# Who reads the split weight tile before a weight sum's DMA, and at which loads the values' sums are issued, in a hybrid decoder block

## The chip, the cores and the metric

One core of a Trainium2 chip runs the kernel in one launch. The metric is the device time of the whole program in microseconds, the median of several executions. Beside the times there is one profiled execution, with a page of summary views and a trace that can be asked for its waits, its chain, its transfers and any stretch of its timeline.

## The reference

The reference is one decoder layer on a sequence of 256 tokens with a model width of 1024. It is cut here to what matters for the order of the work:

```python
proj = jnp.einsum('bsd,dn->bsn', x, w_in)                  # 1024 x 9216 weights
hq, hf, hi, hg, mq, mk, mv, gate_logits = jnp.split(proj, offsets, axis=-1)
o_a = hgrn2_mixer(hq, hf, hi, lb)                          # gated linear recurrence, 8 heads
y_a = rms_norm(o_a, hgrn_norm_w) * silu(hg)
y_b = moba_attention(apply_rope(mq), apply_rope(mk), mv)   # causal attention, 8 heads
z_a, z_b = y_a @ w_branch_a, y_b @ w_branch_b
g_a, g_b = split(sigmoid(gate_logits + b_gate), 2)
x = layer_norm(DN_ALPHA * x + (g_a * z_a + g_b * z_b) @ w_out, ln1_w, ln1_b)
h_gate, h_up = split(x @ w_ffn_in, 2)
return layer_norm(DN_ALPHA * x + (silu(h_gate) * h_up) @ w_ffn_down, ln2_w, ln2_b)
```

All of it is float32. The two projections that this case touches are `hg` (columns 3072 to 4095 of `w_in`), the gate of the recurrence, and `mv` (columns 6144 to 7167), the values of the attention.

## The kernel before

**Weights.** All weights lie in HBM as blocks of 128 x 2048 float32, 1 MB each, in the array `wts`. The kernel walks a list of 89 loads in a fixed order; `stage` (L222 to L250) does one. The SP queue issues the DMA of the block into a tile `raw` (L238; three buffers, so the load three places on is issued when the split of this one is done), ScalarE casts it into a rounded high part `wh` (L243), and VectorE subtracts to get the low part `wl` (L245). `wh` and `wl` have four buffers each, so load n+4 writes the buffers of load n (further on they shift by two, where two loads have tiles of their own). TensorE multiplies with high and low parts for float32 accuracy. I call the cast and the subtraction the split of a load.

**Fewer products.** The gate projection, the values projection and the down projection are done as 2 x 2 block products with seven instead of eight block multiplications (L619 to L658 for gate and values). Some of their right sides are sums and differences of quarters of the weights, called `u1` to `u4`. These sums are not made by an engine but by DMA: the GpSimd queue copies one weight block into a scratch block in HBM, and then copies another block onto it with an adding DMA (L264, `accum_op`). A product that needs `u3` then simply loads it like any other block (`raw<-u` in the profile, `raw<-in_wts_dram` for the plain ones). The list `SUMS` names eight steps for a full set of sums; the gate projection has eight, the values projection four (`u3` copied, `u2` copied, a block added to `u3`, then `u3` added to `u2`), and the down projection sixteen. They are 28 in all, and I number them 0 to 27 in the order of issue: 0 to 7 for the gate, 8 to 11 for the values, 12 to 27 for the down projection.

**When a sum is issued.** `SUMS_WITH` holds 28 load numbers. When `stage` has split load n and n stands in that list, it calls `sum_weights` with the first column of `wl` (L249, L250). That function lets VectorE copy this column of 128 numbers into a small tile `ticks` (L261), lets GpSimd add the tick to itself into `mark` (L262), and puts the DMA behind it on GpSimd's queue (L264). The value of `mark` is never used: the addition is there so that GpSimd's queue stands still until that load is split, and the DMA is not issued before. The additions and DMAs of GpSimd stay in the order in which they are written (`keep_in_program_order`). Where a sum reads what an earlier sum wrote, GpSimd's queue waits for that DMA to land before it issues the next.

The loads that matter here are: 14, 15, 17 and 22, the gate's `u1`, `u3`, `u2` and `u4`; 26 (values `u3`) and 28 and 33 (values `u2`), which need sums 10 and 11; 18, a plain block for the gate; 64 to 71 in the feed-forward part; and 74 on, the down projection.

**Order of the work.** The program is built by a scheduler that simulates a timeline (L1128) and orders the instructions of each engine by it, except in three stretches written out by hand (`manual_schedule`: the first projection, the end of the branches with the first norm, and the down projection) and for the instructions that are kept in program order. Between about 52 us and 205 us VectorE does the steps of the recurrence (`hgrn_steps`, L486 to L568: the steps `kl`, `Qt`, `Kt`, `Tt`, `SD` in the profile) between the splits of the loads, while TensorE runs the projections `hi`, `gb`, `hg`, `ga`, `mv`, `mk`, `mq`.

Of the kernel before, what the change touches and what calls it, by code (L numbers as in the profile page):

```python
# [10 lines left out]
F32 = mybir.dt.float32  # L11
# [3 lines left out]
ALU = mybir.AluOpType  # L15
PSUM = bass.MemoryType.PSUM

P = 128
# [25 lines left out]
VALUE_PRODUCTS = (11, "u1", "u3", "u2", 22, 21, "u4")  # L44
VALUES_BEHIND = (1, 2, 3, 4)
DOWN_ORDER = (0, 1, 3, 4, "a", 2, 6, "b", "c", 5)
SUMS_WITH = (2, 3, 4, 5, 6, 7, 8, 9, 11, 12, 13, 15,
             38, 39, 40, 41, 56, 57, 58, 59, 60, 61, 62, 63, 64, 65, 66, 67)
SUMS = (("u3", 12), ("u1", 11), ("u2", 11), ("u3", 22, "add"), ("u1", 12, "add"), ("u4", 21),
        ("u2", "u3", "add"), ("u4", "u2", "add"))  # L50
# [99 lines left out]
def hybrid_layer_kernel(ctx: ExitStack, tc, x, xw, vecs, wts, ln1_w, ln1_b, ln2_w, ln2_b, consts, out):  # L150
    nc = tc.nc
    pool = lambda name, bufs, **kw: ctx.enter_context(tc.tile_pool(name=name, bufs=bufs, **kw))
    cp = pool("cp", 1)
# [14 lines left out]
    def r32(ap):  # L168
        return ap.bitcast(F32)
# [31 lines left out]
    _, loads, sums = plan()  # L201
    mixed_weights = {}

    def source(at):
        if not isinstance(at, tuple):
            return wts[at]
        if at not in mixed_weights:
            mixed_weights[at] = tc.dram_tile([P, 2048], F32, name=f"{at[3]}_{at[2]}_{at[1]}")
        return mixed_weights[at]
# [12 lines left out]
    def stage(pieces=None, eng=nc.vector):  # L222
        i = state["next"]
        if i >= len(loads):
            return
        state["next"] += 1
        at, k, held = loads[i]
        src = source(at).rearrange("p (k c) -> p k c", k=k)
        view = lambda z: z.rearrange("p (k c) -> p k c", k=k)
        home, tag = (late, "late") if state.get("four") and i % 4 == 0 else (wraw, "raw")  # L230
        raw = view(home.tile([P, 2048], F32, tag=tag, name=f"raw{i}"))
        if held is True:
            h, l = view(slot(f"wh{i}", F32R)), view(slot(f"wl{i}", F32R))
        else:
            h = view(whi.tile([P, 2048], F32R, tag="h", name=f"wh{i}"))
            l = view(wlo.tile([P, 2048], F32R, tag="l", name=f"wl{i}"))
        for ks in ks_of(pieces or (k,)):
            load = nc.sync.dma_start(raw[:, ks, :], src[:, ks, :])  # L238
            if i < EARLY:
                tc.keep_in_program_order(load)  # L240
            if held == "onto":
                nc.vector.tensor_add(raw[:, ks, :], raw[:, ks, :], state["raw"][:, ks, :])
            nc.scalar.copy(h[:, ks, :], raw[:, ks, :])  # L243
            yield
            eng.tensor_sub(l[:, ks, :], raw[:, ks, :], r32(h[:, ks, :]))  # L245
            yield
        state["raw"] = raw
        ready.append((h, l))
        for _ in range(SUMS_WITH.count(i)):  # L249
            sum_weights(r32(l[:, 0, 0:1]))  # L250

    mark = cp.tile([P, 1], F32, tag="mark", name="mark")
    ticks = cp.tile([P, len(sums)], F32, tag="ticks", name="ticks")

    def sum_weights(behind):


        n = len(SUMS_WITH) - len(sums)
        dst, src, add = sums.pop(0)
        tick = ticks[:, n:n + 1]  # L260
        nc.vector.tensor_copy(tick, behind)  # L261
        tc.keep_in_program_order(nc.gpsimd.tensor_tensor(mark, tick, tick, op=ALU.add))  # L262
        more = dict(accum_op=ALU.add, max_dma_last_dim=2048) if add else {}
        tc.keep_in_program_order(nc.gpsimd.dma_start(source(dst), source(src), **more))  # L264

# [728 lines left out]
    for j in range(EARLY, NF, 2):  # L994
        n = j // 2 % 2
# [138 lines left out]
```

## Time and profile before

| | |
|---|---|
| median of 3 runs (lowest to highest) | 491.88 us (491.52 to 492.25) |
| the profiled execution's own time | 492.5 us |
| its span, first to last instruction | 490.7 us |
| TensorE (PE) busy | 482.1 us, 98% of the span |
| VectorE (DVE) busy | 402.9 us, 82% |
| ScalarE (ACT) busy | 318.3 us, 65% |
| GpSimd (POOL) busy | 60.1 us, 12% |

The profiled execution lies 0.6 us above the median. Of its time 1.8 us lie outside the span. Times in the views are in us from the start of the span. In a row of the timeline the first number is the start, the second the length; the bracket at the end is the idle time of that engine before it and what ended it. The letter q behind an engine's name means its queue (a DMA issue or a wait, not work). Instructions follow one another in a pipeline, so a row can begin a little before the one ahead of it has ended.

### The profile page before, as it was taken

How to read it: one execution, taken by the hardware profiler on the slowest of the kernel's cores; microseconds unless marked ns; L12 is line 12 of the kernel's file. 1: busy time of each engine (PE TensorE's matmuls, PEld its weight loads, DVE VectorE, ACT ScalarE, POOL GpSimd, SP SyncE). 2: the span in 40 equal slices, each digit the busy share in tenths (PEclk: the TensorE clock that was granted, in tenths of full speed). 3: DMA queues.
4: the chain of work that ended last, by engine and by line, in shares of the span. 5: the costliest groups of instructions: out<-in, count | busy, mean ns of one | idle time of the engine just before them, and what ended most of it. 6: DMA issues, size and time to landing. Idle time of an engine off the chain costs nothing.

```text
span 490.7 us, 7353 instructions
## 1 busy us (share of the span) xinstructions
PE 482.1 (98%) x2892; PEld 429.6 (88%) x2892; DVE 402.9 (82%) x496; ACT 318.3 (65%) x453; POOL 60.1 (12%) x81
## 2 busy tenths in 40 slices
PE   9999999999999999999999999999999999999993
PEld 9999888888888998999888888888888888888883
DVE  4888899999899789799875998855886679668796
ACT  5797676765879779689773565444665656568610
POOL 2305150320000010001010000001213011000000
PEclk9999999999999999999999999999999999999998
DMA  8979999999957764859767276249999999979902
GB/s 298 387 267 427 280 290 346 285 350 327 296 220 253 285 230 178 311 199 343 257 258 258 85 262 242 97 176 410 282 309 353 316 310 306 294 284 385 344 1 87
DMA packets 23986, 133.60 MB, mean 272 GB/s; under 512 B 2352, under 2 KB 2480, under 8 KB 12336
## 3 DMA queue, kind: packets, MB, share of 16 engines
q1 hardware_dynamic: 15264, 100.63, 53.8%
q0 software_dynamic: 8688, 32.51, 25.8%
q8 instruction: 23, 0.38, 0.3%
q14 instruction: 11, 0.09, 0.1%
HBM read 132.08 MB, written 30.41 MB: 331 GB/s over the span
## 4 chain that ended last, share of the span: by engine, by line
PE 85%; DVE 10%; DMA 2%; issue 1%; ACT 1%; DVEq 0%
PE fu L323 7%; PE fg L323 7%; DVE wl L245 4%; PE fg L324 3%; PE fu L324 3%; PE zb L323 3%; PE za L323 3%; PE ga L323 2%; PE wd L1037 2%; PE wd L1039 2%; PE wd L1038 2%; DMA raw<-in_wts_dram 2%; PE hf L395 2%; PE hf L396 2%; PE hq L367 2%; PE hq L366 2%
## 5 line engine op out<-in xcount | busy, mean ns | idle before, releaser
L245 DVE TENSOR_TENSOR wl<-raw,wh 128x2048 fp32r<-128x2048 f32 x89 | 202.7, 2290 | 54.4 <-ACT wh L243 54.3
L243 ACT CAST wh<-raw 128x2048 fp32r<-128x2048 f32 x89 | 169.5, 1914 | 61.0 <-PE fg L323 17.5
L323 PE MATMUL fg<-x1p,wh 128*128 128x512 f32 x144 | 50.5, 394 | 0.0
L323 PE MATMUL fu<-x1p,wh 128*128 128x512 f32 x144 | 50.4, 394 | 0.0
L324 PE MATMUL fg<-x1p,wl 128*128 128x256 f32 x144 | 40.0, 277 | 0.0
L324 PE MATMUL fu<-x1p,wl 128*128 128x256 f32 x144 | 39.9, 277 | 0.0
L262 POOL TENSOR_TENSOR mark<-ticks 128x1 f32<-128x1 f32 x28 | 21.5, 768 | 134.7 <-DVE ticks L261 111.8
L323 PEld LDWEIGHTS fu<-x1p,wh 128*128 128x128 f32 x144 | 27.0, 187 | 6.2
L323 PEld LDWEIGHTS fg<-x1p,wh 128*128 128x128 f32 x144 | 27.0, 187 | 6.1
L324 PEld LDWEIGHTS fg<-x1p,wl 128*128 128x128 f32 x144 | 27.0, 188 | 0.1
L324 PEld LDWEIGHTS fu<-x1p,wl 128*128 128x128 f32 x144 | 27.0, 188 | 0.0
L323 PE MATMUL za<-yP,wh 128*128 128x512 f32 x64 | 23.6, 405 | 0.0
L323 PE MATMUL ga<-xP,wh 128*128 128x512 f32 x64 | 22.8, 398 | 0.0
L323 PE MATMUL gb<-xP,wh 128*128 128x512 f32 x64 | 22.7, 397 | 0.0
L323 PE MATMUL zb<-yb,wh 128*128 128x512 f32 x64 | 22.3, 394 | 0.0
L365 PE MATMUL mq<-xP,wh 128*128 128x256 f32 x64 | 18.6, 290 | 0.0
L367 PE MATMUL mk<-xP,wl 128*128 128x256 f32 x64 | 18.5, 289 | 0.0
L264 POOL DMA_DIRECT2D u<-in_wts_dram x21 | 17.2, 817 | 10.0 <-DMA u<-in_wts_dram 7.9
L365 PE MATMUL mk<-xP,wh 128*128 128x256 f32 x64 | 18.4, 287 | 0.0
L324 PE MATMUL za<-yP,wl 128*128 128x256 f32 x64 | 18.3, 285 | 0.0
L366 PE MATMUL mq<-xP,wh 128*128 128x256 f32 x64 | 18.2, 284 | 0.0
L366 PE MATMUL mk<-xP,wh 128*128 128x256 f32 x64 | 18.2, 284 | 0.0
(339 smaller groups left out, 1360.0 us busy)
## 6 DMA issues: line engine op xcount, KB each, us to landing
raw<-in_wts_dram SPq DMA_DIRECT2D x74, 1024.0 KB, 6.5
raw<-u SPq DMA_DIRECT2D x15, 1024.0 KB, 7.3
u<-in_wts_dram POOLq DMA_DIRECT2D x7, 1024.0 KB, 17.1
u<-u POOLq DMA_DIRECT2D x7, 1024.0 KB, 17.7
first<-in_xw_dram SPq DMA_DIRECT2D x6, 640.0 KB, 9.7
xr<-in_x_dram POOLq DMA_DIRECT2D x1, 1024.0 KB, 5.4
wb<-in_ln_w_dram POOLq DMA_DIRECT2D x2, 512.0 KB, 6.3
wb<-in_ln_b_dram POOLq DMA_DIRECT2D x2, 512.0 KB, 7.7
```

The source lines that it names most:

```text
L243: nc.scalar.copy(h[:, ks, :], raw[:, ks, :])
L245: eng.tensor_sub(l[:, ks, :], raw[:, ks, :], r32(h[:, ks, :]))
L262: tc.keep_in_program_order(nc.gpsimd.tensor_tensor(mark, tick, tick, op=ALU.add))
L264: tc.keep_in_program_order(nc.gpsimd.dma_start(source(dst), source(src), **more))
L323: nc.tensor.matmul(ps, wh[:, k, wcol], a.both(k), start=(k == 0), stop=False)
L324: last = nc.tensor.matmul(ps[:, 0, :], wl[:, k, wcol], a[0, k, slice(0, T)], start=False, stop=(k == KC - 1))
L365: nc.tensor.matmul(ps, wh[:, k, wcol], ah[:, kk, :], start=(kk == 0), stop=False)
L366: nc.tensor.matmul(ps, wh[:, k, wcol], al[:, kk, :], start=False, stop=False)
L367: nc.tensor.matmul(ps, wl[:, k, wcol], ah[:, kk, :], start=False, stop=(kk == KC - 1))
L395: nc.tensor.matmul(pss[f], wh[:, wcol], xTh[:, k, :], start=(k == 0), stop=False)
L396: nc.tensor.matmul(pss[f], wh[:, wcol], xTl[:, k, :], start=False, stop=False)
L1037: nc.tensor.matmul(ps, lh[:, k, :], wh[:, k, ns], start=n < 5 and i + k == 0, stop=False, **go)
```

## The change

Two things are changed. `sum_weights` no longer copies the column into `ticks`: GpSimd's addition reads the column of `wl` itself, as both of its inputs. And four entries of `SUMS_WITH` move: the values' four sums (8 to 11) were paced by loads 11, 12, 13 and 15, and are now paced by loads 13, 15, 17 and 20. The other 24 entries, the sums and their order stay as they are.

```diff
-SUMS_WITH = (2, 3, 4, 5, 6, 7, 8, 9, 11, 12, 13, 15,
+SUMS_WITH = (2, 3, 4, 5, 6, 7, 8, 9, 13, 15, 17, 20,
              38, 39, 40, 41, 56, 57, 58, 59, 60, 61, 62, 63, 64, 65, 66, 67)
...
-    ticks = cp.tile([P, len(sums)], F32, tag="ticks", name="ticks")
...
     def sum_weights(behind):
-        n = len(SUMS_WITH) - len(sums)
         dst, src, add = sums.pop(0)
-        tick = ticks[:, n:n + 1]
-        nc.vector.tensor_copy(tick, behind)
-        tc.keep_in_program_order(nc.gpsimd.tensor_tensor(mark, tick, tick, op=ALU.add))
+        tc.keep_in_program_order(nc.gpsimd.tensor_tensor(mark, behind, behind, op=ALU.add))
         more = dict(accum_op=ALU.add, max_dma_last_dim=2048) if add else {}
         tc.keep_in_program_order(nc.gpsimd.dma_start(source(dst), source(src), **more))
```

## The prediction

> **What bounds the kernel.** I read the page first, then the waits of TensorE, then the chain of waits around the one place where TensorE waited, then the busy time by stretch.
>
> ```profile
> PE 482.1 (98%) x2892; PEld 429.6 (88%) x2892; DVE 402.9 (82%) x496; ACT 318.3 (65%) x453; POOL 60.1 (12%) x81
> ```
>
> A busy TensorE could still be slow, so the share alone says little. The waits of TensorE over the whole span are two rows:
>
> ```profile
> PE warm L437 <- PEq L1121: 0.8, 1, 0.8
> PE hg L341 <- ACT wh L243: 0.5, 1, 0.5
> ```
>
> One is the launch, which the change does not reach. The other is 0.5 us, once, and it is all the waiting that a change in the feeding of weights could take away. The chain of waits shows where it comes from:
>
> ```profile
> 105.30 2.17 DVE wl L245
> 107.47 0.03 DVE gb L336
> 107.50 9.78 DMA raw<-in_wts_dram
> 117.27 0.02 issue
> 117.30 1.91 ACT wh L243
> 119.21 0.04 issue
> 119.25 0.50 PE hg L341
> ```
>
> Read backwards: the gate's product at 119.25 waits for the cast of its block, the cast for the block's DMA (load 18 by count), and the DMA was issued at 107.50, when the split of load 15 freed a `raw` buffer. The timeline of TensorE shows the gap:
>
> ```profile
> 117.72 1.05 PE L526 MATMUL sc<-Qt,kl 128*128 128x128 f32 x8
> 119.25 0.50 PE L341 MATMUL hg<-wh,xP 128*128 128x512 f32 x1 [0.47 <-ACT wh L243]
> ```
>
> By stretch (PE, PEld, DVE, ACT, POOL busy, clock, DMA share, GB/s), from 53 us to that DMA's issue, to 120 us, and then where the values' sums will be needed:
>
> ```profile
> 53.00:107.50 54.50, 54.50 (x292) 46.84 (x291) 53.80 (x59) 37.43 (x40) 13.40 (x13) 1.00 1.03 322
> 107.50:120.00 12.50, 12.03 (x72) 10.47 (x72) 11.65 (x16) 6.82 (x9) 2.11 (x1) 1.00 1.07 313
> 140.00:156.00 16.00, 16.00 (x88) 13.79 (x87) 16.00 (x19) 12.81 (x16) 0.00 (x0) 1.00 0.51 190
> ```
>
> TensorE is full in each, but for 53 to 107.5 us VectorE is full too, 53.80 of 54.50, and the DMA engines are at their most loaded (1.03). So this stretch has two bounds that lie half a microsecond apart, and everywhere else TensorE alone sets the time. A gain can come only from this half microsecond; a loss needs a new wait of TensorE.
>
> **The change, part by part.**
>
> *The 28 tick copies go.* What one takes from VectorE is the step from its start to the next start:
>
> ```profile
> 66.02 0.14 DVE L261 COPY ticks<-wl 128x1 f32<-128x1 f32 x1
> 66.08 4.48 DVE L245 TENSOR_TENSOR wl<-raw,wh 128x2048 fp32r<-128x2048 f32 x2
> ```
> ```profile
> L261 DVE COPY ticks<-wl x6: 134/138/148, 66.0 to 96.7; 128x1 f32<-128x1 f32 x6
> ```
>
> That is 0.06 us; six lie in the full stretch (the second row is for 53 to 107 us), so 0.36 us there. The other 22 lie where TensorE alone is the bound and are worth nothing.
>
> *New waits.* `wl` now has one more reader, GpSimd, so the split of load n+4, which overwrites it, must wait for the addition of load n. Queued behind that split on VectorE are the recurrence steps and the copies out of PSUM, and TensorE waits for those. The price of a wait that is already fulfilled is bounded by the waits that the splits have now:
>
> ```profile
> L245 DVEq EVENT_SEMAPHORE x90: 21/50/2368, 22.1 to 467.2; - x90
> L245 DVE TENSOR_TENSOR wl<-raw,wh x89: 2269/2291/2331, 23.2 to 470.7; 128x2048 fp32r<-128x2048 f32 x89
> L262 POOL TENSOR_TENSOR mark<-ticks x28: 183/202/4310, 38.1 to 403.3; 128x1 f32<-128x1 f32 x28
> ```
>
> Zero if it shares the existing wait, 0.05 us if it is one more. Seven splits in the full stretch (loads 7 to 13, behind the additions of 3 to 9) then take 0.35 us. I take 0.05, and the two edits cancel: 0.36 less, 0.35 more.
>
> *Is the wait fulfilled in time?* The addition comes right behind its split and is late only when GpSimd's queue stands at a DMA that waits for an earlier sum to land. After sum 7 (load 9) the next addition in the queue belongs to load 13, whose buffer load 17 wants back, far later. The one tight place is near the end:
>
> ```profile
> 402.59 1.01 POOL L264 DMA_DIRECT2D u<-u  x1 [17.68 <-DMA u<-u]
> 403.25 1.89 POOL L262 TENSOR_TENSOR mark<-ticks 128x1 f32<-128x1 f32 x1
> ```
> ```profile
> 408.39 2.29 DVE L245 TENSOR_TENSOR wl<-raw,wh 128x2048 fp32r<-128x2048 f32 x1
> ```
>
> The queue stood 17.68 us for sum 24. Only then came load 67's addition, done at 405.14; load 71 overwrites that buffer at 408.39. The cover is 3.2 us, so the cost is nothing. If that sum landed more than 3.2 us later, VectorE would stand, and with it the copies out of PSUM.
>
> *The port.* The addition read SBUF before (the tick) and still does, 128 numbers.
>
> ```profile
> 66.31 4.31 POOL L262 TENSOR_TENSOR mark<-ticks 128x1 f32<-128x1 f32 x1 [13.20 <-DVE ticks L261]
> ```
>
> This one lasted as long as the two splits that ran from 66.08 to 70.56, while no split of the 89 was over 2.33 us. So VectorE holds GpSimd up and not the reverse, and I set the cost for VectorE at nothing (at most 0.04 us a split). The Trainium skill's page "SBUF — State Buffer", section "Who interferes with whom", says that a VectorE instruction with two SBUF inputs and a GpSimd instruction that reads SBUF exclude each other, and that the one issued first holds the port for its whole length. The trace agrees for the held addition (4.31 us); no split here shows the other half.
>
> *The values' sums move.* Before, sum 10 went out at 105.06 and sum 11 at 121.92:
>
> ```profile
> 105.06 1.04 POOL L264 DMA_DIRECT2D u<-in_wts_dram  x1 [7.85 <-DMA u<-in_wts_dram]
> ...
> 121.92 1.03 POOL L264 DMA_DIRECT2D u<-u  x1 [11.21 <-DMA u<-in_wts_dram]
> ```
>
> Now sum 8 goes with load 13, sum 9 (a plain copy) with load 15 at about 107.7, and sums 10 and 11 with loads 17 and 20:
>
> ```profile
> 114.80 2.28 DVE L245 TENSOR_TENSOR wl<-raw,wh 128x2048 fp32r<-128x2048 f32 x1
> ...
> 128.21 2.28 DVE L245 TENSOR_TENSOR wl<-raw,wh 128x2048 fp32r<-128x2048 f32 x1
> ```
>
> So load 18, in flight from 107.50 to 117.27, has sum 9 beside it in place of sum 10, and the loads ahead of it have one sum fewer beside them and are out of the way sooner. Its 9.78 us must shrink by 0.5 for the wait to go. Bounds: a load has taken 13.8 us beside several sums; downwards nothing excludes the gain, but it is capped at 0.5 by the wait itself.
>
> ```profile
> raw<-in_wts_dram SPq DMA_DIRECT2D x1, 1024.0 KB, 13.8
> ```
>
> I take a little under 9.3 us, from the nearest row, its own 9.78, with one sum less in the neighbourhood.
>
> Moved later, the sums come nearer to their readers. Transfer times in the order of sums 10, 11, and the longest of either kind that I use as bounds (sums 4 and 24):
>
> ```profile
> u<-in_wts_dram POOLq DMA_DIRECT2D x1, 1024.0 KB, 16.4
> ```
> ```profile
> u<-u POOLq DMA_DIRECT2D x1, 1024.0 KB, 17.7
> ```
> ```profile
> u<-in_wts_dram POOLq DMA_DIRECT2D x1, 1024.0 KB, 24.3
> ```
> ```profile
> u<-u POOLq DMA_DIRECT2D x1, 1024.0 KB, 28.6
> ```
> ```profile
> 146.09 0.33 SPq L238 DMA_DIRECT2D raw<-u  x1
> ```
> ```profile
> 155.04 0.33 SPq L238 DMA_DIRECT2D raw<-u  x1
> ```
>
> Sum 10 goes at 117.1 + 0.2 and lands at 117.3 + 16.4 = 133.7 (141.6 with 24.3); its reader, load 26, is issued at 146.09. Sum 11 waits for load 20's split (130.5) and for sum 10, so it lands at 133.7 + 17.7 = 151.4; its reader, load 28, is issued at 155.04. The cover is 3.6 us, and the DMA engines are half idle there (share 0.51). I take no cost. Behind sum 11 on GpSimd's queue stand the additions of the recurrence's norm (L568), which wait for VectorE in any case; from 140 to 156 us GpSimd does nothing (0.00).
>
> *Sum.* VectorE in the full stretch 0, load 18 -0.47, the rest 0. The profiled execution goes from 492.5 to 492.0; it stands 0.6 above the median, so the median goes from 491.88 to 491.4. A measurement of this kernel can tell about 0.2% (1.0 us) from no change, so this is no change.
>
> **The rivals.**
>
> *Nothing moves*: load 18 takes as long beside sum 9 as it did beside sum 10. For it: the DMA share is over 1 on both sides of 107.5. 491.9 us.
>
> *Load 15's split comes later, and the change is slower.* The scheduler orders VectorE anew, with 28 instructions fewer and other waits. If it puts one more recurrence step ahead of that split, load 18 is issued that much later, and with VectorE full nothing absorbs it:
>
> ```profile
> L528 DVE COPY_PREDICATED SD<-cst,sc 128x512 f32<-128x512 uint32 x5 | 6.0, 1197 | 0.0
> ```
>
> One such step is 1.2 us, a long one 2.3 (as the splits), so 493.1 to 494.2 us. It decides from 1.0 us on. Against it: the steps depend on one another, and six ticks of 0.06 us are little to reorder by.
>
> *Load 18 takes longer*, 13.8 us in place of 9.78: 4.0 us more, 495.9.
>
> *Sum 11 lands too late.* With both long transfers it lands at 141.6 + 28.6 = 170.2, 15.2 us after load 28 wants to go, and every later load stands behind that on SP. TensorE's margin on load 28 is the time from the end of its split to the first use of its low part:
>
> ```profile
> 164.34 2.29 DVE L245 TENSOR_TENSOR wl<-raw,wh 128x2048 fp32r<-128x2048 f32 x1 [3.39 <-ACT wh L243]
> ```
> ```profile
> 175.07 0.39 PE L344 MATMUL mv<-wl,xSh 128*128 128x512 f32 x1
> ```
>
> That is 8.4 us, so TensorE waits 6.8 us and the time is 498.7. It decides from a landing at 163.5.
>
> *The addition holds the split.* Now that it comes without a copy in between, it may start ahead of the next split and keep it off SBUF for its own length, 0.2 us (median 202 ns). Seven in the full stretch make 1.4 us: 491.4 + 1.4 = 492.8. The 28 additions before read SBUF as well and lengthened no split, which speaks against it. This is the other half of what the Trainium skill states in "SBUF — State Buffer", section "Who interferes with whom".
>
> *More than the wait goes*: a new order may also let TensorE's own steps follow one another more closely. The waits speak against it, since they show nothing beyond the 0.5. If it decides, it gives over 1.0 us in all: 490.8.
>
> **How the numbers follow.** Forecast (491.4, its own range 490.9 to 491.9) 0.50; nothing moves 0.18; load 15's split later 0.14; load 18 longer 0.05; sum 11 late 0.04; additions holding splits 0.03; more than the wait 0.06. Faster 0.06, same 0.68, slower 0.26. The range 490.8 to 494.2 leaves out the far ends of the last rivals, about 1 in 7.
>
> **What would show it.** Right: no tick rows, the additions read `wl`, TensorE's wait for `wh` in `hg` under 0.3 us or gone, load 18 landing under 9.3 us after an issue near 107.5, sums 10 and 11 issued near 117 and 134, load 28 issued near 155. Wrong: any other wait row of TensorE, a split of VectorE that waits for `mark`, or load 18 issued after 108.5.

## The result and the profile after

The changed kernel takes 495.36 us (median; 493.74 to 496.74), the kernel before in the same session 491.95 us. The ratio is 1.0065, with a 95% interval of 1.0053 to 1.0077: slower by 3.4 us, where 0.5 us less had been forecast. The profiled execution took 495.04 us, its span is 493.3 us against 490.7.

The page of the changed kernel shows the same busy times as before, 1.7 us less for VectorE:

```profile
PE 482.7 (98%) x2892; PEld 429.8 (87%) x2892; DVE 401.2 (81%) x468; ACT 318.2 (65%) x453; POOL 55.6 (11%) x81
```

The difference is in the waits of TensorE (in us in total, times, longest):

```profile
PE sd L497 <- DVE kqh L484: 2.0, 1, 2.0
PE warm L433 <- PEq L1117: 0.8, 1, 0.8
PE hf L391 <- ACT whf L215: 0.3, 1, 0.3
```

The wait of `hg` for its weights is gone, as forecast. A new one has come at another place: the products `sd` of the recurrence wait 2.0 us for `kqh`, which VectorE makes. (Line numbers after the change are four lower from L257 on: L497 is L501 of the kernel before, L484 is L488.) The timeline of TensorE, changed kernel:

```profile
72.82 0.39 PE L409 MATMUL hi<-wl,xP 128*128 128x512 f32 x1
75.24 1.79 PE L497 MATMUL sd<-kqh,ones 128*128 128x512 f32 x4 [2.03 <-DVE kqh L484]
76.83 0.63 PE L319 MATMUL gb<-xP,wh 128*128 128x512 f32 x1
```

The last row shows a second loss: a product of 512 columns is listed with 0.63 us, where the same form had 0.39. The stretches around it (PE, PEld, DVE, ACT, POOL busy, then the granted clock, DMA share, GB/s) show the clock:

```profile
68.00:72.80 4.80, 4.80 (x22) 3.97 (x22) 4.80 (x3) 2.97 (x2) 1.98 (x1) 1.00 1.12 432
72.80:75.80 3.00, 0.97 (x4) 0.52 (x3) 2.94 (x3) 1.97 (x2) 2.44 (x3) 0.96 0.87 360
75.80:79.20 3.40, 3.40 (x11) 2.78 (x11) 3.40 (x4) 2.80 (x5) 0.00 (x0) 0.53 1.01 337
79.20:83.00 3.80, 3.80 (x24) 3.28 (x23) 3.77 (x6) 2.10 (x2) 0.00 (x0) 1.00 1.14 233
```

For 3.4 us right after the wait TensorE had 0.53 of its clock, which costs 3.4 x 0.47 = 1.6 us. So the span can be added up: 2.0 for the wait, 1.6 for the clock, 0.5 less for the wait of `hg` that went, 3.1 in all. The two spans differ by 2.6, because TensorE had come to this place 0.5 us sooner than in the kernel before, the 0.3 us of `hf`, at the start, included: its last product ahead of `sd` began at 72.82, there at 73.32 (further down).

Where does the late `kqh` come from? The chain of waits of the changed kernel, from 37 us to the products:

```profile
37.22 13.32 DMA raw<-in_wts_dram
...
50.57 1.92 ACT wh L243
...
52.56 2.29 DVE wl L245
54.85 1.14 DVE xSl L216
55.99 2.21 DVE Qt L488
...
72.90 2.30 DVE kqh L484
75.19 0.04 issue
75.24 0.94 PE sd L497 x2
```

Load 6 took 13.32 us. Its split stands ahead of `Qt`, the first step of the recurrence, in VectorE's order, and from `Qt` on VectorE works without a gap to `kqh`. In the kernel before `Qt` had waited for ScalarE's `Qg` instead and began 2.4 us sooner:

```profile
53.54 2.29 DVE L492 TENSOR_TENSOR Qt<-Qg,Fg 128x2048 f32<-128x2048 f32 x1 [2.02 <-ACT Qg L458]
```

So only 2.4 us of the load's delay reach `Qt`. Load 6 took 5.9 us there (first row: changed, second: before; the last number is the time to landing):

```profile
raw<-in_wts_dram SPq DMA_DIRECT2D x1, 1024.0 KB, 13.3
```
```profile
raw<-in_wts_dram SPq DMA_DIRECT2D x1, 1024.0 KB, 5.9
```

Both were issued at about the same time. What changed is GpSimd's queue around that moment. Before (the first three rows are VectorE: the splits of loads 2 and 3, a step, and the tick copy of load 2):

```profile
32.85 4.49 DVE L245 TENSOR_TENSOR wl<-raw,wh 128x2048 fp32r<-128x2048 f32 x2 [1.36 <-ACT wh L243]
37.26 0.69 DVE L351 TENSOR_TENSOR xs<-xTr 128x512 f32<-128x512 f32 x1
37.86 0.15 DVE L261 COPY ticks<-wl 128x1 f32<-128x1 f32 x1
```
```profile
37.37 0.33 SPq L238 DMA_DIRECT2D raw<-in_wts_dram  x1
```
```profile
38.09 0.57 POOL L262 TENSOR_TENSOR mark<-ticks 128x1 f32<-128x1 f32 x1 [19.00 <-DVE ticks L261]
38.60 0.70 POOL L264 DMA_DIRECT2D u<-in_wts_dram  x1
39.32 2.37 POOL L262 TENSOR_TENSOR mark<-ticks 128x1 f32<-128x1 f32 x1
39.45 2.66 POOL L264 DMA_DIRECT2D u<-in_wts_dram  x1
```

After:

```profile
37.22 0.33 SPq L238 DMA_DIRECT2D raw<-in_wts_dram  x1
```
```profile
35.07 2.17 POOL L258 TENSOR_TENSOR mark<-wl 128x1 f32<-128x1 f32 x1 [16.65 <-DVE wl L245]
37.19 0.70 POOL L260 DMA_DIRECT2D u<-in_wts_dram  x1
37.91 0.54 POOL L258 TENSOR_TENSOR mark<-wl 128x1 f32<-128x1 f32 x1
38.39 0.53 POOL L260 DMA_DIRECT2D u<-in_wts_dram  x1
```

Sum 0 now goes out at the very moment at which load 6 does, 1.4 us sooner, and sum 1 1.1 us sooner. The tick copy of load 2 had stood behind load 3's split and a step of `xs` in VectorE's order, and had held sum 0 back. Without it the addition starts at 35.07, right behind load 2's split, but lasts 2.17 us, until load 3's split (34.91 to 37.20) is done. The end of that same split frees the `raw` buffer for load 6, so sum 0 and load 6 now leave together: in all six programs here without this tick and with sum 0 at load 2, sum 0 goes 0.03 us ahead of load 6.

And the kernel before had almost no room for a late `kqh`: there it was done 0.6 us before TensorE came to `sd`.

```profile
70.66 2.29 DVE L488 TENSOR_TENSOR kqh<-Qg,kqh 64x2048 fp32r<-64x2048 f32 x1
```
```profile
73.32 0.39 PE L413 MATMUL hi<-wl,xP 128*128 128x512 f32 x1
73.55 0.39 PE L501 MATMUL sd<-kqh,ones 128*128 128x512 f32 x1
```

### The profile page after: what moved, and what is told of

Same layout as the page of the kernel before. It is cut to its first block, busy times and chain, and to the rows that moved or that the text cites. A ratio compares the mean times of both kernels' runs of the same rounds, so it can differ in the third digit from the quotient of the medians.

```text
span 493.3 us, 7349 instructions
## 1 busy us (share of the span) xinstructions
PE 482.7 (98%) x2892; PEld 429.8 (87%) x2892; DVE 401.2 (81%) x468; ACT 318.2 (65%) x453; POOL 55.6 (11%) x81
## 4 chain that ended last, share of the span: by engine, by line
PE 83%; DMA 7%; DVE 4%; ACT 3%; issue 2%; SPq 0%; DVEq 0%; ACTq 0%
PE fu L319 7%; PE fg L319 7%; DMA raw<-in_wts_dram 6%; PE fg L320 3%; PE fu L320 3%; PE gb L319 3%; PE zb L319 3%; PE za L319 3%; PE ga L319 3%; PE wd L1033 2%; PE wd L1035 2%; PE wd L1034 2%; PE sc L522 2%; PE gb L320 2%; DVE wl L245 2%
## 5 line engine op out<-in xcount | busy, mean ns | idle before, releaser
L258 POOL TENSOR_TENSOR mark<-wl 128x1 f32<-128x1 f32 x28 | 16.9, 603 | 170.5 <-DVE wl L245 164.1
L320 PE MATMUL gb<-xP,wl 128*128 128x256 f32 x64 | 18.5, 289 | 0.0
L361 PE MATMUL hq<-xP,wh 128*128 128x256 f32 x64 | 18.1, 283 | 0.0
```

The lines of the kernel that those rows point to most:

```text
L258: tc.keep_in_program_order(nc.gpsimd.tensor_tensor(mark, behind, behind, op=ALU.add))
L320: last = nc.tensor.matmul(ps[:, 0, :], wl[:, k, wcol], a[0, k, slice(0, T)], start=False, stop=(k == KC - 1))
L361: nc.tensor.matmul(ps, wh[:, k, wcol], ah[:, kk, :], start=(kk == 0), stop=False)
```

## The experiments

Three theories were put against each other. A: without the ticks sums 0 and 1 go out with load 6, it lands late, the recurrence comes late, TensorE waits, and its clock falls. B: the values' sums, moved later, cost the time. C: GpSimd's reading of `wl` costs it, by the new wait of the splits or by the port. Each run is compared with runs of the kernel before on its own chip.

**Sum 0 one load later.** The changed kernel with

```diff
-SUMS_WITH = (2, 3, 4, 5, 6, 7, 8, 9, 13, 15, 17, 20,
+SUMS_WITH = (3, 3, 4, 5, 6, 7, 8, 9, 13, 15, 17, 20,
```

> The changed kernel, with the first sum paced by load 3 in place of load 2 (so sums 0 and 1 both go after the split of load 3, behind the issue of load 6's DMA). Theory A (the copies on VectorE had held sums 0 and 1 back behind load 6's DMA; without them load 6 lands 7 us later and the recurrence comes late): load 6 lands about 6 us after its issue, not 13.3; TensorE's wait for kqh at 73 us goes, the clock row has no 0.5 between 70 and 80 us; 491.2 to 491.9 us. Theory B (the values' sums, moved later, cost the time) and theory C (the split's new wait for GpSimd, or GpSimd's reading of wl, costs it): 495, as the changed kernel.

Measured: 491.96 us, ratio 0.9992 (0.9984 to 1.0001). Sum 0 went at 37.44, 0.57 us after load 6's issue instead of with it; load 6 took 8.4 us (about 6 expected), `kqh` was done at 72.4, and beside the launch TensorE waits only once, 0.4 us for a cast at `mv`.

So one number in the list gives the whole loss back, with all reads of `wl` and the values' late sums in place. B and C cannot explain that. (The scheduler also moved a few other instructions; the run with short packets, further down, keeps the order.)

**The two edits apart.** First the kernel before with only the values' sums moved:

```diff
-SUMS_WITH = (2, 3, 4, 5, 6, 7, 8, 9, 11, 12, 13, 15,
+SUMS_WITH = (2, 3, 4, 5, 6, 7, 8, 9, 13, 15, 17, 20,
```

> The kernel before with only the values' four sums moved to loads 13, 15, 17 and 20; the copies into ticks stay. Theory A: no slower, and load 18 lands in under 9.3 us so that TensorE's wait of 0.5 us goes: 491.3 to 491.9. Theory B: 495. Theory C: as A.

Measured: 491.55 us, ratio 0.9988 (0.9980 to 0.9997). Load 18 took 5.0 us, and the launch is the only wait of TensorE that is left.

Then the changed kernel with the values' sums at their old loads:

```diff
-SUMS_WITH = (2, 3, 4, 5, 6, 7, 8, 9, 13, 15, 17, 20,
+SUMS_WITH = (2, 3, 4, 5, 6, 7, 8, 9, 11, 12, 13, 15,
```

> The changed kernel with the values' four sums back at loads 11, 12, 13 and 15; GpSimd reads wl itself. Theory A: load 6 lands about 13 us after its issue, TensorE waits about 2 us for kqh near 73 us, and the time is 494 to 496. Theory B: 491.9. Theory C: 494 to 496 as well, with a wait of a split for mark in VectorE's waits; without such a row C falls.

Measured: 494.25 us, ratio 1.0045 (1.0028 to 1.0061). Load 6 took 13.7 us, and TensorE's wait of 2.0 us for `kqh` is back. No split waits for `mark` in VectorE's waits. B falls: the moved sums are worth a tenth of a per cent, as a gain.

**The tick on another engine.** The kernel before with

```diff
-        nc.vector.tensor_copy(tick, behind)
+        nc.scalar.copy(tick, behind)
```

> The kernel before with the copy into ticks moved from VectorE to ScalarE; GpSimd reads ticks and never wl, the values' sums are where they were. ScalarE is idle when load 2 is split, so sum 0 should go at about 35.5 to 37.5 us, ahead of load 6's DMA. Theory A: load 6 lands late again (over 10 us after its issue) and the time is 494 to 496, though GpSimd does not touch wl. Theory C: no slower than 491.9 plus what 28 copies cost ScalarE, which is not the bound. If the copy lands behind a cast on ScalarE, sum 0 goes later and A too expects 491.9: the issue times of sum 0 and of load 6 decide which.

Measured: 491.27 us, ratio 0.9984 (0.9975 to 0.9993). Sum 0 went at 37.4, 0.6 us after load 6 (issued 36.8), which took 9.0 us; `kqh` was in time. (Its profiled execution, 492.52 us, has another wait of TensorE, 1.5 us for VectorE at `ga`.) So this is the second branch of the expectation. The copy landed behind other work of ScalarE, and the run tells only that taking the 28 copies off VectorE does no harm by itself.

**One tick of 28.** The kernel before with

```diff
-        nc.vector.tensor_copy(tick, behind)
+        if n:
+            nc.vector.tensor_copy(tick, behind)
+        else:
+            tick = behind
```

> The kernel before with one of the 28 copies taken out, that of sum 0, whose addition reads wl itself; all others and the values' sums stay. Theory A: sum 0 goes within 0.3 us of load 6's issue, load 6 lands over 10 us after it, TensorE waits about 2 us for kqh: 494 to 496. Theory C (the splits' new waits, or the reads of wl, 28 of them): one of 28, so 492.0.

Measured: 492.54 us, ratio 1.0026 (1.0000 to 1.0051), and no single time: of ten executions six took 491.2 to 492.6 us, three 495.3 to 496.8 and one, which the ratio leaves out, 499.66, while 21 of the kernel before on that chip lay between 491.29 and 492.95. In the profiled one (492.45 us) sum 0 went at 37.1 with load 6, which took 11.0 us, as A expected; but the scheduler had put `kqh` ahead of the split of load 9 here, and it was done at 70.65, so TensorE did not wait. A half confirmed: one tick is enough to make the load late. That the order behind it spared TensorE is seen in this execution alone; why four others of the same program took 3 us more and over is not shown.

**Sum 1 later, sum 0 as in the changed kernel.**

```diff
-SUMS_WITH = (2, 3, 4, 5, 6, 7, 8, 9, 13, 15, 17, 20,
+SUMS_WITH = (2, 4, 4, 5, 6, 7, 8, 9, 13, 15, 17, 20,
```

> The changed kernel with sum 0 still at load 2 but sum 1 at load 4 in place of 3, some 3 us later. It tells which of the two sums holds load 6 up. If sum 0 alone does (it stands just ahead of load 6 on the DMA engines): load 6 still lands 11 us or more after its issue and the time is 494 to 496. If both are needed: load 6 lands in 6 to 9 us and the time is 491.3 to 492.0.

Measured: 496.05 us, ratio 1.0085 (1.0071 to 1.0099). Load 6 took 8.3 us, so by the landing both sums are needed to hold it up for 13; but the time did not come back. The chain shows why. It begins one load further on:

```profile
41.86 12.60 DMA raw<-in_wts_dram
...
54.54 1.92 ACT wh L243
...
56.48 2.29 DVE wl L245
58.77 2.21 DVE Qt L488
```

In this program the scheduler put the split of load 7 ahead of `Qt` too, and load 7, which has the sums beside it in every version, took 12.6 us; TensorE waited 2.8 us for `kqh`. I had expected one of two times by the landing of load 6 alone and was wrong: what counts is the landing of whichever load stands last ahead of `Qt`.

**Short packets.** Is a load late because of the bytes beside it, or because of how they are cut? The DMA queues of the changed kernel from 38 to 46 us (packets, MB, share of 16 engines):

```profile
q0 software_dynamic: 48, 2.10, 62.6%
q1 hardware_dynamic: 201, 1.47, 44.6%
```

SP's queue (q1) moved 1.47 MB in 201 packets, 7 KB each, and by its share of the time one holds an engine for 44.6% x 16 x 8 us / 201 = 0.28 us. GpSimd's queue (q0) moved 2.10 MB, two sums. How a sum is cut shows where one stands alone, in the kernel before from 37.3 to 43.3 us:

```profile
q0 software_dynamic: 16, 1.05, 48.2%
```

So a sum is 16 packets of 66 KB, and one holds an engine for 48.2% x 16 x 6 us / 16 = 2.9 us. In the changed kernel's view 32 of the 48 packets carry the two sums (the others next to nothing), and one holds an engine for 62.6% x 16 x 8 us / 32 = 2.5 us. The changed kernel, with the plain sums cut as the adding ones are:

```diff
-        more = dict(accum_op=ALU.add, max_dma_last_dim=2048) if add else {}
+        more = dict(accum_op=ALU.add, max_dma_last_dim=2048) if add else dict(max_dma_last_dim=2048)
```

> The changed kernel with the plain copies of the sums cut into rows of 2048 numbers (8 KB), as the adding ones are; before, a copy of 1 MB goes as 16 packets of 64 KB that hold a DMA engine for 2.4 to 3.4 us each, against 0.3 us for a packet of a load. The sums go out as early as in the changed kernel. If load 6 is late because its packets stand behind these long ones in turn (theory A with that mechanism): load 6 lands in under 10 us, the wait for kqh goes, 491.2 to 492.2. If it is late because of the bytes alone (the same 2 MB read and written beside it): it lands after 12 us or more as in the changed kernel, 494 to 496.

Measured: 491.26 us, ratio 0.9989 (0.9980 to 0.9998), faster than both kernels. The instructions of TensorE, VectorE and ScalarE stand in exactly the order of the changed kernel, sum 0 again goes with load 6 (36.99 and 37.02), and nothing but the packets differs:

```profile
q1 hardware_dynamic: 240, 1.70, 54.8%
q0 software_dynamic: 362, 1.42, 45.3%
```
```profile
raw<-in_wts_dram SPq DMA_DIRECT2D x1, 1024.0 KB, 6.7
```

Load 6 lands in 6.7 us, loads 7 and 8 in 9.6 and 8.5 (13.7 and 12.8 in the changed kernel), and TensorE has no wait but the launch. A packet of GpSimd's queue now has 3.9 KB and holds an engine for 0.16 us. This settles why load 6 was late: same order, same moment of issue, same sums. What held it up were long packets among its short ones. With the cut GpSimd's queue also moves less beside the load, 1.42 MB from 38 to 46 us for 2.10; the two come with one edit, and the run does not tell them apart. The Trainium skill's page "DMA: Bandwidth & Descriptors", section "Queues, rings and completion order", says that an engine takes turns between the queues that have work for it and changes only when a whole packet is through. These two runs agree: beside packets of 2.5 us the load took 13.3 us, beside packets of 0.16 us 6.7.

The same edit to the kernel before, where the sums go behind load 6 anyway:

> The kernel before with the plain copies of the sums in rows of 8 KB; the copies into ticks and the early values' sums stay. The sums stay behind load 6, so theory A sees no loss to undo: 491.2 to 492.0; loads 7 to 9, which took 12.5 to 13.8 us beside the long packets, land in 8 to 10 us. Whether load 18's wait of 0.5 us goes too is open: sum 10, beside it, was in 8 KB rows already, sums 8 and 9 ahead of it were not.

Measured: 491.63 us, ratio 0.9997 (0.9985 to 1.0010), with the order of the kernel before. Loads 7 to 9 took 9.3, 8.6 and 8.8 us; load 18 took 9.6 us, and 0.3 us of its wait stayed. So short packets undo a loss where there is one and are no gain of their own that these runs can tell from noise.

**The margin, without any DMA.** The kernel before with one more step on VectorE:

```diff
         nc.vector.tensor_mul(kq, flat(Kt), kq)
+        nc.vector.tensor_mul(kqt, flat(Kt), flat(Kt))
```

> The kernel before with one more VectorE instruction of 2.3 us ahead of the steps that end in kqh (a product into a buffer that is overwritten next, so the result is the same); ticks, sums and their times are not changed. In the kernel before kqh was ready 0.6 us before TensorE came to need it. If that margin is all there is (theory A): kqh comes 2.3 us later, TensorE waits 1.5 to 2 us for it, and the time is 493.4 to 495.2, the upper end where the clock falls to half for 3.4 us as in the changed kernel. If there was slack that absorbs it: 491.9 to 492.3.

Measured: 496.96 us, ratio 1.0098 (1.0083 to 1.0112), above the expected range. The wait for `kqh` is what the margin says: `kqh` came 1.6 us later (72.26 for 70.66), TensorE came to it 0.5 us sooner, and of these 2.1 us it waited 1.4. But a second one has joined it, for ScalarE's copies of `hi` out of PSUM:

```profile
PE gb L323 <- ACT hv L614: 2.2, 1, 2.2
PE sd L502 <- DVE kqh L488: 1.4, 1, 1.4
```

and the clock was at half for 6.8 us. A margin of 0.6 to 0.7 us is borne out; the price per microsecond behind it is higher than I had put it.

**The clock.** The changed kernel with TensorE given 2 us more to do, ahead of `sd`:

```diff
+        fill = aux.tile([P, 512], F32, tag="aux", name="fill")
+        for i in range(9):
+            nc.tensor.matmul(fill, ones, xSh[:, 0], start=i == 0, stop=i == 8)
         for g in range(4):
             ps = aux.tile([P, 4, P], F32, tag="aux", name=f"sd{g}")
```

> The changed kernel with nine further products of 512 columns (2.05 us of TensorE) ahead of the product that waits for kqh; their result goes nowhere. They add work to TensorE in front of the wait and so fill it. Theory A (a wait of 2 us, and then a clock at half speed for 3.4 us, which costs another 1.5): the wait shrinks below 0.4 us, the clock row has no 0.5 near 85 us, and the time falls by about 1.5 us to 493.9, although TensorE has 2 us more to do. Rival (the clock row costs nothing, the wait is the whole loss): the time stays at 495.4. Rival (TensorE's work alone sets the time, the wait was hidden): 497.4.

Measured: 495.04 us, ratio 1.0066 (1.0052 to 1.0079). It decides nothing. The scheduler put the nine products at 51 to 53 us, over 20 us ahead of the wait:

```profile
L495 PE MATMUL fill<-xSh,ones x9: 389/389/398, 51.0 to 52.8; 128*128 128x512 f32 x9
```

They made TensorE come to `sd` 1.8 us later, but load 6 took 16.0 us here and `kqh` came 2.0 us later than in the changed kernel, so the wait was 2.3 us. The clock stayed at 1.00 this time. That the fall of the clock follows from the wait is therefore seen, in the changed kernel, but not shown by an experiment of its own.

## Why the prediction was wrong

*The bound.* Right: TensorE alone sets the time, a gain could come only from the 0.5 us, and a loss needed a new wait of TensorE. There was one. Two readings on the way were wrong and carried nothing: the DMA engines' share is not highest in the full stretch (1.03; the next row has 1.07), and sums 4 and 24 are not the longest of their kinds (sum 21 took 24.9 us, sum 25 32.1).

*The ticks: the step that failed.* "The other 22 lie where TensorE alone is the bound and are worth nothing." I priced a tick by the 0.06 us that it takes from VectorE and not by what stood behind it: the addition, and behind the addition a DMA of 1 MB. The tick of load 2 waited in VectorE's order for the split of load 3 and a step of `xs`, and this was what put sum 0 behind load 6. Taking the ticks out moved the DMAs of the gate's eight sums; I worked out new times only for the values' four, whose entries the diff moves in plain sight. In place of nothing the runs show 7.4 us on the landing of load 6, 2.2 us on `kqh` and 2.0 us of wait, and 1.6 us of clock.

*What could have been seen.* The margin of 0.6 us between `kqh` and `sd` stands in the trace of before. I looked for waits of TensorE, found the one at 119 us and the full stretch of VectorE from 53 us on, and did not ask for each product that needs VectorE how long ahead its operand was ready. The full stretch of VectorE ends its first part at `kqh`, 45 us ahead of the place that I watched.

*New waits and the port.* Right. The waits of the splits and the splits in the changed kernel:

```profile
L245 DVEq EVENT_SEMAPHORE  x109: 21/49/2368, 21.9 to 469.6; - x109
L245 DVE TENSOR_TENSOR wl<-raw,wh x89: 2267/2291/2314, 23.0 to 473.3; 128x2048 fp32r<-128x2048 f32 x89
```

There are 19 waits more (109 for 90) of 0.05 us, none that VectorE stood at for `mark`, and no split was longer than before (2314 ns at most, for 2331). That VectorE holds GpSimd's addition up has a consequence that I left out: the addition of load 2, held for 2.17 us, put sum 0 at the moment of load 6.

*The tight place near the end.* Right: load 67's addition was done at 407.72, load 71's split began at 410.97, 3.3 us of cover for 3.2.

*The values' sums.* Right. Load 18 landed in 4.7 us and its wait went. Sums 10 and 11 went at 117.86 and 132.43 (117 and 134 expected), sum 11 landed at 148.4, and load 28 was issued at 158.38, freed by a split and not by the sum. The run of this edit alone came out 0.6 us faster (ratio 0.9988), against the 0.47 of the forecast's sum.

*The rivals.* The one that put a late step of VectorE against the forecast had the kind of loss right but its place and its cause wrong. Load 18 was issued at 109.54, 2.0 us later and past the 108.5 that I had named as a sign of being wrong, but only because all work behind the wait came later: the same steps stand ahead of load 15's split in both kernels. The other rivals did not happen.

## What to carry to other kernels

A small instruction that paces a DMA is worth what it delays, not what it lasts: before it goes, list the DMAs behind it, their new issue times, and the transfers that they now meet. Where one engine is full, look up for every consumer of its results how long ahead the operand was ready; a bound engine without a wait can still be half a microsecond from one. And where a background copy must share the DMA engines with loads that are waited for, cut it into packets as short as theirs.

## What the hardware showed

**Order at the DMA engines.** Half a microsecond of issue time moved a load by several. With sum 0 issued 1.2 us after load 6 the load took 5.8, 5.9 and 6.6 us (three programs), 0.6 us after it 8.4 and 9.0, and at the same moment, with sum 1 1.2 us later, 13.3, 13.7 and 16.0. Sum 1 counts too: with sum 0 at the same moment and sum 1 1.8 us after the load it took 11.0 us, with sum 1 5.4 us after it 8.3. With short packets, at the same moment and sum 1 1.2 us later, it took 6.7.

**The clock after a short wait.** In the profile of the changed kernel a wait of 2.0 us was followed by 3.4 us at 0.53 of the clock. In the run with the values' sums early, an equal wait was not:

```profile
73.70:76.10 2.40, 0.45 (x3) 0.03 (x1) 2.34 (x2) 1.38 (x1) 2.40 (x3) 1.00 0.94 369
76.10:79.50 3.40, 3.37 (x17) 2.73 (x18) 3.39 (x3) 3.39 (x6) 0.03 (x1) 1.00 1.02 364
```

The same stretch after the wait holds 17 products here and 11 there. A wait of 2.8 us in the run with sum 1 later was followed by a fall (0.50 from 78 to 80 us), one of 2.3 us in the run with the added products was not. The Trainium skill's page "TensorE: Matmul & The Clock Gate", section "Part 1: The HAM clock gate (the "warmup" mystery)", says that the clock is halved after an idle window of about 3.4 us, and that these windows run freely. The length agrees (3.4 us, and 6.8 us with two waits); that the wait alone must be as long as a window does not, since 2.0 us were enough. The measurement decides: a wait of 2 us may or may not cost another 1.6.

The mean granted clock of each execution, which was taken with its time, bears out this price. A fall to 0.53 for 3.4 us takes 3.4 x 0.47 / 493 = 0.003 off the mean. The 64 executions of the kernel before that the experiments were compared with had 0.994 to 0.998. Of the six of the changed kernel, two had 0.995 and took 493.74 and 494.17 us; the other four had 0.992 or 0.993 and took 495.04 to 496.74. With the values' sums early, five had 0.995 or 0.996 and took 493.69 to 494.49 us, and the one with 0.992 took 496.26. So much of the spread of 3.0 us goes with the clock, and without its fall the changed kernel still stands some 2 us behind the kernel before.
